# Tile pairs with one multiply, 16 tiles transposed on VectorE and loaded by quarters, and plain tiles loaded far ahead, in a matmul with rotary embedding

## The chip, the cores and the metric

One core of one Trainium2 chip; the other cores are idle. Times are microseconds on the device, of whole executions. A profile's span, from the first to the last instruction, is 1.7 to 1.8 us shorter than the time of the same execution. Engines: PE is TensorE, DVE VectorE, ACT ScalarE, POOL GpSimd, SP SyncE, which here only issues DMAs. A suffix q (SPq, ACTq) stands for an engine's instruction queue where it issues DMAs.

## The reference

```python
# x (16, 512, 768), weight (768, 768), cos and sin (512, 64), 12 heads; all float32
y = np.matmul(x, weight).reshape(batch, seq, n_heads, 64)
y1, y2 = y[..., :32], y[..., 32:]
out1 = y1 * cos1 - y2 * sin1          # cos1, sin1: first halves, the same for all heads
out2 = y2 * cos2 + y1 * sin2
out = np.concatenate([out1, out2], axis=-1).reshape(batch, seq, hidden)
```

## The kernel before

64 tiles of 128 rows by 768. Each is loaded on SP, cast to fp16 on ScalarE, transposed on TensorE (six times 128x128, into PSUM), evicted by ScalarE, multiplied by the weights (12 matmuls), multiplied twice on VectorE (by cos and by the signed sin), added on GpSimd, and stored by a DMA that ScalarE issues.

```python
    def load(i):
        xss[i] = xpool.tile([P, H], FP32, tag="xs", name="xs")             # 11 buffers
        nc.sync.dma_start(out=xss[i], in_=xv[i // SB, i % SB])
    ...
    def transpose(i, eng):
        xc = x16.pop(i)
        pt = pt_pool.tile([P, NKT, P], FP16, tag="pt", name="pt")
        for kt in range(NKT):
            nc.tensor.transpose(pt[:, kt, :], xc[:, ts(kt, P)], ident)
        xTT[i] = tpool.tile([P, NKT, P], FP16, tag="xT", name="xT")
        copy(eng, xTT[i], pt)
    ...
    def store(i):
        nc.scalar.dma_start(out=ov_dram[i // SB, i % SB], in_=ovs.pop(i))
    ...
    for i in range(FIRST, NMB):
        if i + AHEAD - FIRST < NMB:
            load(i + AHEAD - FIRST)
        if i + 1 < NMB:
            transpose(i + 1, nc.scalar)
        if 4 < i + 2 < NMB:
            cast(i + 2, nc.scalar)
        if i < NMB - 1:
            for kt in range(NKT):
                mm(i, kt)
            rope_whole(i)           # two multiplies on VectorE, one add on GpSimd
            store(i - 3)
```

## Time and profile before

| | before |
|---|---|
| time | 168.62 us (3 runs, 168.53 to 168.65) |
| span of the profiled run | 166.9 us, granted clock 0.983 |
| TensorE busy | 153.6 us; no wait between 21.4 and 160.1 us |
| a tile in the steady stage | 2.285 us: 1.95 matmul, 0.34 transposes |
| DMA | 53.2 MB, 319 GB/s over the span |
| DMAs in the steady stage | two a tile: one load, one store, 384 KB each |

The lines behind this table are in the prediction.

### The profile page before, as it was taken

To read this page: it belongs to the slowest core of one execution; us is meant where nothing else is said; L and a number is where in the kernel's file an instruction comes from. 1 tells how busy PE (TensorE), PEld (TensorE's weight loads), DVE (VectorE), ACT (ScalarE), POOL (GpSimd) and SP (SyncE) were. 2 spreads that over 40 slices of the span, in tenths; PEclk is the share of its full clock that TensorE was granted. 3 is DMA by queue.
4 is the path that set the end of the run, shared out by engine and by line. 5 is a ranking of instruction groups with operands and counts; after the bars stand their busy time and mean duration, and the time that the engine had idled before them with its cause. 6 is when DMAs were issued, how large, how long until landed. Compare 5 with 4: busy or idle time off the path is not lost.

```text
span 166.9 us, 3136 instructions
## 1 busy us (share of the span) xinstructions
PE 153.6 (92%) x1165; PEld 98.5 (59%) x1165; DVE 122.9 (74%) x142; ACT 97.9 (59%) x127; POOL 114.4 (69%) x67
## 2 busy tenths in 40 slices
PE   7657699999999999999999999999999999999930
PEld 2224466666666666666666666666666666666610
DVE  0522598777877688877778877778877778777792
ACT  3053366667766667766667766667666667666400
POOL 0000099777787777887777887777887777877770
PEclk9987999999999999999999999999999999999997
DMA  4999999999999999999999999999999984345544
GB/s 128 405 402 403 403 404 369 301 375 406 340 372 343 328 350 345 350 326 381 335 327 370 347 330 351 337 327 361 368 349 350 300 323 170 146 161 192 213 166 188
DMA packets 19887, 53.19 MB, mean 319 GB/s; under 512 B 2336, under 2 KB 2848, under 8 KB 19872
## 3 DMA queue, kind: packets, MB, share of 16 engines
q1 hardware_dynamic: 10368, 27.92, 49.5%
q10 hardware_dynamic: 9504, 25.07, 37.8%
q8 instruction: 9, 0.15, 0.5%
q14 instruction: 6, 0.05, 0.1%
HBM read 27.82 MB, written 25.17 MB: 317 GB/s over the span
## 4 chain that ended last, share of the span: by engine, by line
PE 88%; DMA 4%; ACT 2%; DVE 2%; issue 1%; SPq 1%; DVEq 0%
PE psy L103 74%; PE pt L93 13%; DMA xs<-in_x_dram 4%; PE psy L216 1%; DVE ov L130 1%; ACT xc L69 1%; ACT xT L69 1%; DVE qv L122 1%; SPq L80 1%; DVE tv L116 0%; SPq L75 0%; DVEq L130 0%; DVEq L116 0%
## 5 line engine op out<-in xcount | busy, mean ns | idle before, releaser
L130 POOL TENSOR_TENSOR ov<-tv,qv 128x768 f32<-128x768 f32 x63 | 114.2, 1816 | 47.4 <-DVE qv L122 46.2
L103 PE MATMUL psy<-w_sb,xT 128*128 128x512 f16 x756 | 135.1, 329 | 2.5 <-ACT xT L69 1.8
L103 PEld LDWEIGHTS <-xT 128*128 128x128 f16 x756 | 71.8, 99 | 44.9 <-ACT xT L69 2.1
L116 DVE TENSOR_TENSOR tv<-psy,cos_sb 128x768 f32<-128x768 f32 (+1 forms) x65 | 61.4, 944 | 31.7 <-PE psy L103 30.5
L69 ACT COPY xT<-pt 128x768 f16<-128x768 f16 x63 | 50.3, 798 | 51.2 <-PE pt L93 51.2
L122 DVE TENSOR_TENSOR qv<-psy,tee_sb 128x768 f32<-128x768 f32 (+1 forms) x65 | 60.7, 934 | 0.0
L69 ACT CAST xc<-xs 128x768 f16<-128x768 f32 x63 | 52.7, 836 | 5.8 <-DMA xs<-in_x_dram 5.8
L93 PE MATMUL pt<-ident,xc 128*128 128x128 f16 x384 | 31.9, 219 | 2.9 <-ACT xc L69 2.2
L93 PEld LDWEIGHTS <-xc 128*128 128x128 f16 x384 | 26.6, 98 | 12.3 <-ACT xc L69 3.0
L83 DVE CAST w_sb<-w_raw 128x768 f16<-128x768 f32 x6 | 3.3, 558 | 4.1 <-DMA w_raw<-in_weight_dram 4.1
L141 PE MATMUL cold_ps<-cold 128*128 128x512 f16 x13 | 4.6, 514 | 1.2 <-DVE cold L146 1.2
L141 PEld LDWEIGHTS <-cold 128*128 128x128 f16 x13 | 1.5, 126 | 3.3 <-issue 1.9
L71 DVE CAST xc<-xs 128x768 f16<-128x768 f32 x1 | 0.6, 560 | 3.7 <-DMA xs<-in_x_dram 3.7
L69 ACT ACT_TABLE_LOAD x1 | 1.3, 1283 | 2.1 <-issue 2.1
L216 PE MATMUL psy<-w_sb,xT 128*128 128x384 f16 x12 | 2.1, 326 | 0.0
L130 DVE TENSOR_TENSOR ov<-tv,qv 128x384 f32<-128x384 f32 x2 | 1.7, 862 | 0.1
L216 PEld LDWEIGHTS <-xT 128*128 128x128 f16 x12 | 1.2, 98 | 0.8
L71 DVE COPY xT<-pt 128x768 f16<-128x768 f16 x1 | 0.6, 556 | 0.6 <-PE pt L93 0.6
L146 DVE MEMSET cold<- 128x256 uint32 x1 | 0.3, 272 | 0.9 <-PEq L244 0.9
L244 POOL MEMSET const-float32-0.0<- 128x1 f32 x1 | 0.1, 98 | 0.2 <-issue 0.2
L185 DVE TENSOR_SCALAR tee_sb<-tee_sb 128x128 f32<-128x128 f32 x1 | 0.2, 220 | 0.0
L244 POOL MEMSET const-bfloat16-1.0<- 128x1 bf16 x1 | 0.1, 101 | 0.0
(2 smaller groups left out, 0.2 us busy)
## 6 DMA issues: line engine op xcount, KB each, us to landing
xs<-in_x_dram SPq DMA_DIRECT2D x64, 384.0 KB, 5.6
out_dram<-ov ACTq DMA_DIRECT2D x63, 384.0 KB, 4.8
w_raw<-in_weight_dram SPq DMA_DIRECT2D x6, 384.0 KB, 5.9
out_dram<-ov SPq DMA_DIRECT2D x2, 192.0 KB, 2.2
cos_sb<-in_cos_dram ACTq DMA_DIRECT2D x1, 128.0 KB, 5.2
tee_sb<-in_sin_dram ACTq DMA_DIRECT2D x1, 128.0 KB, 6.2
ident<-identity ACTq DMA_DIRECT2D x1, 32.0 KB, 3.6
```

What stands on the lines that cost most here:

```text
L69: eng.copy(out=o, in_=i_)
L71: eng.tensor_copy(out=o, in_=i_)
L80: nc.sync.dma_start(out=w_raw[:, kt], in_=wv[:, kt])
L83: nc.vector.tensor_copy(out=w_sb[:, kt], in_=w_raw[:, kt])
L93: nc.tensor.transpose(pt[:, kt, :], xc[:, ts(kt, P)], ident)
L103: nc.tensor.matmul(psys[i][:, ds(noff, nsz)], xTT[i][:, kt, :], w_sb[:, kt, ds(noff % H, nsz)], start=(kt == 0), stop=(kt == NKT - 1),)
L116: nc.vector.tensor_tensor(out=tv.rearrange("p (h d) -> p h d", d=D), in0=ps.rearrange("p (h d) -> p h d", d=D), in1=cos_sb[:, sb, :].unsqu ...
L122: nc.vector.tensor_tensor(out=qv.rearrange("p (h t d) -> p h t d", t=2, d=HD), in0=ps.rearrange("p (h t d) -> p h t d", t=2, d=HD)[:, :, : ...
L130: add_eng.tensor_tensor(out=ov[:, ds(c0, n)], in0=tv, in1=qv, op=ADD)
L141: nc.tensor.matmul(cold_ps, cold[:, 0:P], cold, start=True, stop=True)
L146: nc.vector.memset(cold, 0.0)
L216: nc.tensor.matmul(psys[i][:, n, 0:sz], xTT[i][:, kt, :], w_sb[:, kt, ds(c0, sz)], start=(kt == 0), stop=(kt == NKT - 1),)
```

## The change

Its intent: take TensorE transposes off the engine that bounds the kernel. VectorE transposes 16 tiles within 32x32 blocks, on pairs of fp16 seen as one fp32. For that a tile is put into SBUF by quarters of the hidden dimension, so it is loaded by four DMAs of 32 partitions. VectorE gets the time for it from one multiply per pair of tiles, by cos and sin at once, in place of four. The start loads four x tiles ahead of the weights, and early on plain tiles are loaded up to 14 pairs ahead. Cut to the core:

```diff
+    def by_blocks(n, s):                      # pair n, tile s of it
+        return s == 1 and 6 < n < NP - ALONE and n % SB != 0
...
-    xpool = ctx.enter_context(tc.tile_pool(name="xpool", bufs=AHEAD + 3))
+    xpool = ctx.enter_context(tc.tile_pool(name="xpool", bufs=24))
+    bpool = ctx.enter_context(tc.tile_pool(name="bpool", bufs=AHEAD_B + 1))
...
+    def load_blocks(n):
...
+        src = x[b].rearrange("(j a r) (q k) -> r q a j k", r=SB, a=R, q=NQ)
+        dst = xss[n, 1].rearrange("p (j k) -> p j k", j=NQ)
+        for q in (0, 2, 1, 3):
+            eng = nc.sync if q < 2 else nc.scalar
+            eng.dma_start(out=dst[ts(q, R)], in_=src[r, q])
...
+    def transpose_blocks(n, s):
+        xT = tpool.tile([P, NT, P, 2], FP16, tag="xT", name="xT")
+        nc.vector.transpose(
+            out=xT.bitcast(FP32).rearrange("p t m e -> p (t m e)"),
+            in_=x16.pop((n, s)).bitcast(FP32),
+        )
...
+    def rope_pair(n):
+        rope(n, 0, 2 * H, psys[n].rearrange("p b n -> p (b n)"))   # one multiply, 3072 columns
+        add(n, 0, 2 * H, nc.gpsimd)
...
+    for n in range(2, NP):
+        while loaded < min(NP, n + 6 + max(0, AHEAD - n // 3)):
+            load_plain(loaded)
+            loaded += 1
+        if n + 1 < NP and by_blocks(n + 1, 1):
+            transpose_blocks(n + 1, 1)
+        for s in (0, 1):
+            for c in CHUNKS:
+                mm(n, s, *c)
+            upto("turn", 2 * n + s + 3)          # transposes on TensorE, evictions on ScalarE
+            upto("cast", 2 * n + s + 5)
...
+        if n >= 3:
+            store(n - 3, nc.scalar)              # a pair, 768 KB
+        load_blocks(n + AHEAD_B)
+        if n < NP - ALONE:
+            rope_pair(n)
```

## The prediction

What the prediction told of the hardware and no trace or run of this case shows is cut from it, and each cut is marked. The sum came to a span of 150.9 + 7.3 = 158.2 us and, with 1.7 us over it, to 159.9, put down as 159.8. Three things are estimates: that the cast and the weight loads cost no more with strided reads, that transfers of 32 partitions run at the rate of full ones, and that GpSimd slows nothing of VectorE in the tail.

> **What bounds the kernel now.** I read the busy shares first, then the chain of work that ended last, then the same chain in order of time, and the timeline of the first and last 12 us. The shares and the chain:
>
> ```profile
> PE 153.6 (92%) x1165; PEld 98.5 (59%) x1165; DVE 122.9 (74%) x142; ACT 97.9 (59%) x127; POOL 114.4 (69%) x67
> DMA  4999999999999999999999999999999984345544
> ...
> PE 88%; DMA 4%; ACT 2%; DVE 2%; issue 1%; SPq 1%; DVEq 0%
> ```
>
> TensorE is the bound, and nothing else comes near it on the chain. The DMA row looks just as full, and I come back to it. In order of time the chain has three stages:
>
> ```profile
> 15.84 3.10 PE psy L103 x18
> 18.93 0.35 PE pt L93 x6
> 19.33 0.67 issue
> 20.00 0.84 ACT xc L69
> 20.89 0.51 PE pt L93 x6
> 21.40 1.95 PE psy L103 x12
> 23.35 0.34 PE pt L93 x6
> ...
> 158.17 1.96 PE psy L216 x12
> 160.70 0.56 DVE qv L122
> 161.28 1.17 DVE ov L130
> ```
>
> Start: until 21.40 us only three tiles are multiplied and five transposed. Steady stage: a tile costs 1.95 us of matmul and 0.34 us of transposes without a gap; 61 tiles x 1.953 + 59 x 0.338 = 139.1 us, which from 21.4 gives 160.5, and the chain has the last matmul end at 160.13. Tail: 160.13 to 166.9, 6.8 us. So there are three places to gain: the start, the 0.34 us per tile, the tail. The rest of the engines in the steady stage:
>
> ```profile
> L130 POOL TENSOR_TENSOR ov<-tv,qv 128x768 f32<-128x768 f32 x63 | 114.2, 1816 | 47.4 <-DVE qv L122 46.2
> L116 DVE TENSOR_TENSOR tv<-psy,cos_sb 128x768 f32<-128x768 f32 (+1 forms) x65 | 61.4, 944 | 31.7 <-PE psy L103 30.5
> L69 ACT COPY xT<-pt 128x768 f16<-128x768 f16 x63 | 50.3, 798 | 51.2 <-PE pt L93 51.2
> L69 ACT CAST xc<-xs 128x768 f16<-128x768 f32 x63 | 52.7, 836 | 5.8 <-DMA xs<-in_x_dram 5.8
> ```
>
> Of the 2.285 us per tile VectorE fills 1.9 (two multiplies), GpSimd 1.82, ScalarE 1.63: all wait for TensorE, none is far from it.
>
> The DMA row is not a bound yet. Loads alone ran at 402 GB/s; the demand of the steady stage is 786 KB per 2.285 us = 344 GB/s, and the windows of 4 us show 304 to 415. In the trace's packet records a 3 KB packet takes 121 ns in both queues, which for 16 engines is 406 GB/s; 6.6% of the load packets between 60 and 100 us take over 200 ns and make 26% of the load time. I read those as latency of a queue that had run empty, not as lost capacity. No cast waits for x after the start (5.8 us in two waits).
>
> [...]no transpose on VectorE is in this trace. [...]the first add of the last tile (two SBUF inputs) took 1.17 us beside a GpSimd add, the second 0.56 us alone; the multiplies (PSUM and SBUF) stay at 0.95 beside GpSimd. [...]the cast, which now reads pairs of fp32 at a step of 24 bytes[...]: I take the cast as unchanged. [...]All stationary operands of the transposes and those of the block tiles now have a step of 2 elements; the trace only has packed ones, 98 ns each[...]. I take them as unchanged.
>
> **The change part by part.**
>
> *Block transposes.* Pairs 7 to 27 without those divisible by 4 give 16 tiles. Each drops 6 TensorE transposes, 0.338 us on the path: 16 x 0.338 = -5.4 us. Each drops an eviction of 0.80 us on ScalarE, off the path. Each adds one VectorE transpose of 384 fp32: from the multiplies of 768 (0.95 us) and 384 (0.55 us) a column costs 1.03 ns and an instruction 0.16 us, so 0.56 us (an estimate[...]), beside TensorE.
>
> *One multiply per pair.* 3072 columns in place of 4 x 768: 0.16 + 3072 x 1.03 = 3.32 us against 3.80. VectorE per pair with a block tile: 3.32 + 0.56 = 3.88 us of TensorE's 2 x 1.953 + 0.338 = 4.24 us (4.58 without). It fits, with 0.36 us to spare. The PSUM now has two pair buffers: pair n+1 may start when the multiply of pair n-1 is done, 3.32 us after that pair's last matmul; it would start 4.24 us after it. Slack 0.9 us, so no stall. This saves nothing by itself; it pays for the transposes.
>
> *GpSimd.* One add of 1536: at most 2 x 1816 = 3.63 us of 4.24. One input is now read with halves swapped; unchanged rate assumed.
>
> *ScalarE.* Per pair with a block tile 2 x 0.84 + 0.80 + three DMA issues at 0.34 = 3.5 us of 4.24.
>
> *Start.* Order of loads: four x tiles, six weight rows, then cos and sin. Before, x0 was there at 4.83 and each later transfer 0.975 us after the one ahead (weight casts at 9.49, 10.46, and 12.41, 13.39). So w0 lands at 4.83 + 4 x 0.975 = 8.7 and w5 at 13.6, as before. By then 4 tiles are transposed, and each weight needs 0.56 us of cast and at most 3 x 0.325 us of matmul, so TensorE keeps pace: w5 cast by 14.2, matmuls to 15.1, (1,0)'s last to 15.5. The third x pair comes after cos and sin (0.65 us): 15.2, cast 16.05, transposed 16.4. So the fourth tile starts at about 16.4 with five tiles transposed, the very state that the kernel before had at 21.40: -5.0 us. Risk: before, the clock was at half from about 11 to 14.4 us:
>
> ```profile
> PEclk9987999999999999999999999999999999999997
> 10.81 3.80 PE psy L103 x12
> ```
>
> Twelve matmuls took 3.80 us in place of 1.95. The change keeps TensorE warm with extra matmuls, but 7 to 9.3 us is thin; if the slow stretch comes again it costs up to 1.7 us. I add 0.8.
>
> *Steady stage.* 61 x 1.953 + 43 x 0.338 = 133.7 us. From 16.4 + 0.8: last matmul at 150.9.
>
> *Tail.* All transposes are done early, so the last six tiles come every 1.95 us; VectorE needs 0.16 x 2 + 1536 x 1.03 = 1.9 us for each and starts 1.4 us behind (3.32 - 1.95), so it ends some 1.0 us behind. Then three instructions on 512 columns (0.69 each) and three on 256 (0.42): 3.3 us[...]. From the last add (163.97) to the end before were 2.97 us. Tail 1.0 + 3.3 + 3.0 = 7.3, against 6.8: +0.5.
>
> *Sum.* Span 150.9 + 7.3 = 158.2. The time is 1.7 us over the span (168.62 to 166.9): 159.9. I say 159.8; the parts are -5.4, -5.0 + 0.8, +0.5.
>
> **The rivals.** *DMA becomes the bound.* With block tiles the demand is 1.573 MB per 4.24 us = 371 GB/s, and a 768-byte packet should take about 36 ns (1 KB takes 46, 1.5 KB takes 66, 3 KB 121), so 19% more for a quarter-loaded tile: 388 GB/s of 406. For: that is tight[...]. Against: 24 buffers in place of 11 let 13 tiles (5.1 MB) be read ahead, which over some 90 us takes 56 GB/s off[...].[...]
>
> *VectorE or the PSUM becomes the bound.* If the transpose takes 1.0 us rather than 0.56, VectorE needs 4.32 us per block pair, and 16 x 0.1 plus waits cost 2 to 4 us: 163.[...]
>
> *Strided reads cost.* If the cast at a 24-byte step took twice as long, ScalarE would need 5.3 us a plain pair and the kernel would be no faster (170 or more). If strided weight loads doubled a transpose, 48 x 0.34 = 16 us would undo everything: 174. [...]an author who kept this layout over six transposes per tile would have seen it.
>
> *GpSimd.* If swapped halves cost 20%, 4.36 us a pair makes it the bound for 16 pairs: 2 to 3 us.
>
> **Range and chances.** Downward little is left: without the cold stretch and with VectorE on time in the tail 158; so low 156.5. Upward several of the rivals are each worth 2 to 5 us: high 165. Two rivals would make it the same or slower, together some 9%: faster 0.91, same 0.05, slower 0.04.
>
> **What would show it.** Right: the chain stays with TensorE, at about 4.24 us per block pair and 4.58 per plain pair; the first matmul of tile (1,1) at 16 to 18 us; the multiply at 3.3, the transpose at 0.56, the cast at 0.84, the add at 3.6 us or less; weight loads at 98 ns. Wrong: TensorE waiting for the pair multiply or for a cast in pairs 7 to 27 (VectorE, or quarters landing late), a cast over 1 us, an add over 4.2 us, a slow clock after 20 us.

## The result and the profile after

| | before | after |
|---|---|---|
| time | 168.63 us (4 runs, 168.53 to 168.75) | 176.93 us (4 runs, 175.81 to 177.39) |
| ratio of fast runs | | 1.048, 95% interval 1.043 to 1.053 |
| span, granted clock | 166.9 us, 0.983 | 174.9 us, 0.958 |
| TensorE without work between 22 us and its last matmul | 0.0 us | 9.8 us |
| lost there to a low clock | 0.0 us | 4.8 us |

The result is right in its numbers and slower by 4.8%. Ratios here and below are the mean time of one kernel's fast runs over that of the other's of the same rounds, so not quite the ratio of the medians that are quoted. The last two rows are sums over windows of 1 us: the part of a window in which TensorE was not busy, and its busy part times what the granted clock lacked.

The page of the changed kernel, busy shares, slices and chain (four lines of them):

```profile
PE 154.4 (88%) x1074; PEld 94.8 (54%) x1074; DVE 123.8 (71%) x74; ACT 87.5 (50%) x109; POOL 109.2 (62%) x38
...
PE   7899999995895799999689999999999699999900
...
PEclk9999999999699699999969999999999999999995
...
DMA 42%; PE 38%; DVE 6%; ACT 3%; issue 2%; ACTq 2%; SPq 2%; POOL 1%; POOLq 1%; DVEq 0%
```

TensorE has holes at 42, 55, 86 and 139 us, the first three with a dip of the clock behind them: waits of 2.51, 2.89 and 2.00 us were followed by 12 matmuls in 3.58, 3.74 and 3.54 us in place of 2.11, at a granted clock of down to 0.50; after the wait of 1.52 us at 139 us they took 2.11, and in e2 the clock stayed at 1.00 after one of 2.3 us (85.4 to 87.7 us). The chain, 88% TensorE before, now runs over DMAs for 42% of the span. The pieces that were changed did what was expected of them; the groups of instructions by shape:

```profile
L194 POOL TENSOR_TENSOR ov<-tq 128x1536 f32<-128x1536 f32 x29 | 100.2, 3458 | 60.7 <-DVE tq L183 47.7 <-DMA out_dram<-ov 13.0
L183 DVE TENSOR_TENSOR tq<-psy,csn 128x3072 f32<-128x3072 f32 x29 | 97.3, 3356 | 35.1 <-PE psy L169 35.1
L76 ACT CAST xc<-xs 128x768 f16<-128x768 f32 x46 | 40.8, 901 | 8.3 <-DMA xs<-in_x_dram 7.9 <-issue 0.3
L126 PEld LDWEIGHTS <-xc 128*128 128x128 f16 x288 | 20.2, 100 | 11.6 <-ACT xc L76 4.4 <-DVE xc L78 1.2 <-issue 1.1
L133 DVE STREAM_TRANSPOSE xT<-xc 128x384 f32<-128x384 f32 x16 | 9.1, 570 | 2.4 <-ACT xc L76 2.4
```

The column behind the first bar is busy time and mean ns. The multiply takes 3.36 us (3.32 worked out), the block transpose 0.57 (0.56), the add 3.46 (at most 3.63), a strided weight load 100 ns (98 packed), the cast 0.90 (0.84 taken). So did the start; the chain in order of time:

```profile
15.72 0.90 ACT xc L76
...
16.66 0.51 PE pt L126 x6
17.17 1.95 PE psy L169 x12
19.12 0.34 PE pt L126 x6
```

The fourth tile starts at 17.17 us, where 16.4 and 0.8 in reserve had been written. The half-speed stretch before 20 us is gone: between 11 and 14 us the granted clock was 0.50 and is 1.00. From 7 to 11 us TensorE was busy for 42% of the time before, and for 87% in the change.

One hole in detail, from the timeline of the changed kernel (start, duration, instruction; in brackets the idle time of the engine before it and what ended it):

```profile
52.47 0.50 PE L126 MATMUL pt<-ident,xc 128*128 128x128 f16 x6
52.80 2.11 PE L169 MATMUL psy<-w_sb,xT 128*128 128x256 f16 x12
...
54.83 0.41 ACTq L240 DMA_DIRECT2D out_dram<-ov  x1
...
55.28 1.63 ACTq L102 DMA_DIRECT2D xb<-in_x_dram  x2
...
56.95 0.80 ACT L76 COPY xT<-pt 128x768 f16<-128x768 f16 x1 [4.65 <-DMA xs<-in_x_dram]
57.65 0.89 ACT L76 CAST xc<-xs 128x768 f16<-128x768 f32 x1
57.81 3.74 PE L169 MATMUL psy<-w_sb,xT 128*128 128x512 f16 x12 [2.89 <-ACT xT L76]
```

The transposes of a tile are done at 52.97 us. Their eviction, 0.80 us of work, starts only at 56.95, after ScalarE had been idle for 4.65 us; TensorE waits 2.89 us for it, and its next 12 matmuls take 3.74 us, where the 12 above took 2.11, at the low clock (0.50 from 58 to 61 us). ScalarE did not wait for the data of the eviction. Ahead of it in its order stand a store and two quarter loads, and it could not issue them: by the single records of the trace, 2.46 of the 4.65 us passed before the store could be issued and 0.83 before the second quarter could; the three issues themselves took 1.21. The list of the compiled program shows why; first one DMA of SP, then five instructions of ScalarE in order:

```
SP   L83  DMACopy xs_637<-in_x_dram 128x768        [waits DMAHW6, Activation]
...
ACT  L76  TensorCopy xc_625<-xb_519 128x768        [waits DMAHW5, DMAHW6, DMAHW0, Activation]
ACT  L240 DMACopy out_0_dram<-ov_466 128x2x768     [waits DMAHW6, Pool]
ACT  L102 DMACopy xb_628<-in_x_dram 32x4x192       [waits DMAHW1]
ACT  L102 DMACopy xb_628<-in_x_dram 32x4x192       [waits DMAHW3]
ACT  L76  TensorCopy xT_661<-pt_654 128x768        [waits PE]
```

The program has eight completion counters for DMAs, DMAHW0 to 7. They go to the DMAs in turn, in the order of the compiled list, over both queues, and a DMA is not issued until the one eight before it has landed. (All 155 DMAs take the counters in turn, and for each of the 147 after the first eight its engine waits, at it or earlier, for the DMA eight before.) The list is not in the order of the kernel's text: SP's DMAs run ahead of ScalarE's in it. The store takes counter 6 from the load of `xs_637`, which the text issues after the store. The chain in order of time has that load in flight until the store's issue:

```profile
48.62 6.14 DMA xs<-in_x_dram
...
54.83 6.18 DMA out_dram<-ov
...
61.09 6.10 DMA out_dram<-ov
```

Load, store, store: each issue follows the landing of the DMA whose counter it takes. In a stage of four pairs the changed kernel has 4 stores, 5 plain loads and 12 quarters, 21 DMAs in 17.3 us (8 x 1.953 + 5 x 0.338), so on average a DMA must land within 8/21 x 17.3 = 6.6 us of its own issue, or the one that takes its counter is late; the medians to landing are 5.2 to 6.6 us, single ones up to 9.4. Before, it was 16 DMAs in 18.3 us: 9.1 us, with medians of 4.8 and 5.6.

### The profile page after: what moved, and what is told of

It reads as the page before. It is cut to its first block, busy times and chain, and to the rows that moved or that the text cites. A ratio compares the mean times of both kernels' runs of the same rounds, so it can differ in the third digit from the quotient of the medians.

```text
span 174.9 us, 2708 instructions
## 1 busy us (share of the span) xinstructions
PE 154.4 (88%) x1074; PEld 94.8 (54%) x1074; DVE 123.8 (71%) x74; ACT 87.5 (50%) x109; POOL 109.2 (62%) x38
## 4 chain that ended last, share of the span: by engine, by line
DMA 42%; PE 38%; DVE 6%; ACT 3%; issue 2%; ACTq 2%; SPq 2%; POOL 1%; POOLq 1%; DVEq 0%
PE psy L169 32%; DMA out_dram<-ov 16%; DMA xb<-in_x_dram 13%; DMA xs<-in_x_dram 9%; DVE tq L183 6%; PE pt L126 5%; DMA w_raw<-in_weight_dram 4%; ACT xc L76 2%; ACTq L102 1%; POOL ov L194 1%; POOLq L364 1%; ACT xT L76 1%; SPq L83 1%; ACTq L240 1%; SPq L102 1%
## 5 line engine op out<-in xcount | busy, mean ns | idle before, releaser
L194 POOL TENSOR_TENSOR ov<-tq 128x1536 f32<-128x1536 f32 (+1 forms) x34 | 109.0, 3216 | 60.7 <-DVE tq L183 47.7
L169 PE MATMUL psy<-w_sb,xT 128*128 128x512 f16 (+1 forms) x744 | 133.8, 334 | 7.8 <-ACT xT L76 7.8
L183 DVE TENSOR_TENSOR tq<-psy,csn 128x3072 f32<-128x3072 f32 (+2 forms) x35 | 102.6, 2943 | 35.1 <-PE psy L169 35.1
L76 ACT COPY xT<-pt 128x768 f16<-128x768 f16 x46 | 36.5, 799 | 51.3 <-PE pt L126 25.4
L76 ACT CAST xc<-xs 128x768 f16<-128x768 f32 x46 | 40.8, 901 | 8.3 <-DMA xs<-in_x_dram 7.9
L126 PE MATMUL pt<-ident,xc 128*128 128x128 f16 x288 | 24.3, 223 | 3.0 <-ACT xc L76 2.3
L126 PEld LDWEIGHTS <-xc 128*128 128x128 f16 x288 | 20.2, 100 | 11.6 <-ACT xc L76 4.4
L76 ACT CAST xc<-xb 128x768 f16<-128x768 f32 x16 | 14.4, 899 | 7.3 <-DMA xb<-in_x_dram 4.5
L133 DVE STREAM_TRANSPOSE xT<-xc 128x384 f32<-128x384 f32 x16 | 9.1, 570 | 2.4 <-ACT xc L76 2.4
L169 PE MATMUL psz<-w_sb,xT 128*128 128x512 f16 (+1 forms) x24 | 4.2, 326 | 0.0
```

Of the source, the lines that this page charges most:

```text
L76: eng.copy(out=o, in_=i_)
L126: nc.tensor.transpose(pt[:, t, e, :], xc[:, t, e, :], ident)
L133: nc.vector.transpose(out=xT.bitcast(FP32).rearrange("p t m e -> p (t m e)"), in_=x16.pop((n, s)).bitcast(FP32),)
L169: nc.tensor.matmul(ps, xTT[n, s][:, t, e, :], w_sb[:, t, e, lo:hi], start=((t, e) == CHUNKS[0] and not joined), stop=((t, e) == CHUNKS[-1] ...
L183: nc.vector.tensor_tensor(out=tqs[n][:, :, c0:c1].rearrange("p j (h d) -> p j h d", d=D), in0=ps.rearrange("p (h d) -> p h d", d=D) .unsqu ...
L194: eng.tensor_tensor(out=ovs[n][:, ds(c0, w)].rearrange("p (h t d) -> p h t d", t=2, d=HD), in0=tq[:, 0].rearrange("p (h t d) -> p h t d", ...
```

## The experiments

They ran four at a time, each four on one chip, the fours on four different chips (e1 to e4; f1, f2, e5 and h1; f3, j1, j2 and g1; k1 to l2), with the kernel before beside them at medians of 166.8 to 167.1 us. The change itself was not run beside them, so runs of different fours, and the change, are compared by their ratios (the change: 1.048). Theories: **A**, the counters; **B**, slow transfers (packets of 768 bytes, or 32 partitions); **C**, VectorE and the two PSUM buffers too tight; **D**, the far look-ahead, which makes the SP queue deep. (Two counts in the expectations are off: 6.25 DMAs a pair counts quarters for every pair, the stage has 21 in four pairs, 5.25 a pair; and g1 goes from 21 to 19, not from 25 to 23. The 2.0 us from span to time is 1.8 in the runs.) With one core a run is called slow by its time alone. In e1, e3 and k2 half the runs are slow, and the profiled runs of e1 and k2 are among them, so there a slow run may be one in which a stall came and a fast one one in which it did not.

**e1_one_plain**, wrong result:

```diff
-        for q in (0, 2, 1, 3):
-            eng = nc.sync if q < 2 else nc.scalar
-            eng.dma_start(out=dst[ts(q, R)], in_=src[r, q])
+        nc.sync.dma_start(out=xss[n, 1], in_=x[b].rearrange("(p r) h -> r p h", r=SB)[r])
```

> Wrong result on purpose: each of the 16 block tiles is loaded by one transfer of whole 3 KB rows on the SP queue in place of four quarters; cast, VectorE transpose, matmuls and buffers as in the change. Theory A (counters): the instruction list shows that every DMA, of both queues, takes the next of eight completion counters in program order, and its issue waits until the DMA eight before it has landed; four quarters use up four of the eight, so SP and ScalarE stop at issues. With 3.0 in place of 6.25 DMAs a pair the stalls of TensorE after 40 us vanish: 17.2 + 133.7 + 7.3 us span + 2.0 = 160 us. Rival B (packets of 768 B or 32 partitions make transfers slow): also about 160. Rival C (VectorE and the two PSUM buffers are too tight): stays at 173 to 177. Rival D (plain loads far ahead fill the queues): 168 or more.

166.24 us (163.29 to 167.97; the fast runs 165.7 and 163.3), ratio 0.986 (0.975 to 0.996). C falls: with the same VectorE work and the same PSUM buffers, 6% of the time (1.048 to 0.986), some 10 us, is gone. A was too sure of itself: TensorE is still idle for 4.2 us in the profiled run, a slow one, where ScalarE waits 6.8 us once.

**e2_four_whole_rows**, wrong result: four DMAs of 32 partitions, but whole rows of 3 KB.

```diff
-            eng.dma_start(out=dst[ts(q, R)], in_=src[r, q])
+            eng.dma_start(out=xss[n, 1][ts(q, R)], in_=src[ts(q, R)])   # src: rows of 768
```

> Wrong result on purpose: four transfers of 32 partitions on the same queues and in the same order as in the change, but of whole 3 KB rows, so there are no small packets. Theory A (eight counters): as slow as the change, 172 to 178 us. Rival B in its form of small packets: about 160 us; in its form of 32 partitions: slow as A says, which e3 and a later run must part.

175.37 us, ratio 1.052 (1.045 to 1.058); TensorE idle for 11.0 us. As slow as the change without one small packet.

**e3_one_small_packets**, wrong result: one DMA of 128 partitions in pieces of 768 bytes.

```diff
+        src = x[b].rearrange("(p j) (q k) -> q p j k", j=SB, q=NQ)[r]
+        nc.sync.dma_start(out=xss[n, 1].rearrange("p (j k) -> p j k", j=NQ), in_=src)
```

> Wrong result on purpose: one transfer of 128 partitions in four pieces of 768 B each, so small packets as in the change but one counter a tile. Theory A: 160 to 162 us, as e1. Rival B (small packets): near the change, 170 us or more.

165.13 us (fast runs 163.33 and 163.97), ratio 0.981 (0.973 to 0.988). Small packets alone do no harm. A's 160 to 162 us was missed here too: TensorE is idle once, for 1.8 us. In the packet records they take 36 ns, as the prediction had interpolated.

**e4_no_blocks**, correct: `by_blocks` returns False, all else kept.

> Correct result: no block tiles; all tiles transposed on TensorE and loaded plainly, the rest of the change kept (pairs, start, loads far ahead). TensorE has 17.2 + 61 x 1.953 + 59 x 0.338 = 156.3 us, tail 7.3, and 2.0 over the span: 165.6 us under A and B. Under C (pair multiply and PSUM) or D (loads far ahead) it stalls: 170 or more.

170.13 us, ratio 1.018 (1.011 to 1.025). 4.5 us over the sum that A gave, and without a quarter in it. The profile shows one hole, at 57 us: a load that SP had issued at 45.58 took 11.66 us to land, and the store that takes its counter held up ScalarE till 57.26. So quarters are not needed for such a stop; this spoke for D as well.

**f1_near**, correct: the change without the far look-ahead.

```diff
-        while loaded < min(NP, n + 6 + max(0, AHEAD - n // 3)):
+        while loaded < min(NP, n + 6):
```

> Correct result: the change without the far look-ahead of plain loads (pair n+6 is loaded at pair n throughout; the first eight pairs as before); quarters kept. e1, e3 and e4 still stalled TensorE once or twice, behind a store whose counter had last been taken by a load that stood in a deep SP queue. Theory A+D (counters, made worse by the deep queue): fewer stalls than the change, 165 to 172 us. A alone, if only the four quarters matter: 173 to 177. If the look-ahead is what keeps the transfers in time: 178 or more.

173.32 us (fast runs 172.5 to 173.5), ratio 1.036 (1.033 to 1.039), TensorE idle for 9.7 us. The look-ahead is not the cause; by the ratios, 1.048 and 1.036, it costs some 2 us at most.

**f2_near_one_plain**, wrong result: f1 and e1 together.

> Wrong result on purpose: f1 with each block tile loaded by one plain transfer, as in e1. Theory A+D: no stall is left, 17.2 + 133.7 + 8.7 (the tail as e4 showed it) + 2.0 = 161.6 us. If the stalls left in e1 have another cause than the look-ahead: 163 to 166, as e1.

160.79 us (160.49 to 160.97), ratio 0.963 (0.961 to 0.964), TensorE idle for 0.0 us after 22 us. With neither quarters nor the long look-ahead the prediction's 159.8 us holds within 1 us. Part of that is luck: the last matmul ends 0.8 us before the predicted 150.9, the tail is 1.3 us longer, and the ratio forecast was 0.948, as the kernel before is faster on this chip.

**e5_four_columns**, wrong result: four DMAs of all 128 partitions and 192 columns.

```diff
+        src = x[b].rearrange("(p r) (q k) -> r q p k", r=SB, q=NQ)
+        dst = xss[n, 1].rearrange("p (q k) -> p q k", q=NQ)
...
+            eng.dma_start(out=dst[:, q], in_=src[r, q])
```

> Wrong result on purpose: the change with four transfers a block tile, each of all 128 partitions and 192 columns (768 B packets), on the same queues in the same order. Theory A (counters): as slow as the change and e2, 172 to 178 us, as the count is the same. Rival B in its form of 32 partitions: 163 to 166 us, as e3.

175.39 us, ratio 1.051 (1.044 to 1.057). With e2 and e3 this ends B in both forms: neither packets nor partitions matter. What e2 and e5 share with the change, and e3 does not, is four DMAs a tile, two of them issued on ScalarE; j2 below keeps the four and moves the issues.

**h1_before_four**, correct: the kernel before, x loads from tile 8 on in four column pieces.

```diff
-        nc.sync.dma_start(out=xss[i], in_=xv[i // SB, i % SB])
+        k = H // 4 if i >= AHEAD else H
+        for c in range(0, H, k):
+            nc.sync.dma_start(out=xss[i][:, ds(c, k)], in_=xv[i // SB, i % SB, :, ds(c, k)])
```

> Correct result: the kernel before with every x load from tile 8 on split into four transfers of 192 columns on the SP queue; nothing else. Five DMAs a tile of 2.285 us take counters, so a DMA must land within 1.6 tiles, 3.7 us, where it took 4.8 to 5.6. Theory A: slower by 3% or more, with ScalarE waiting at its stores. Rival B (32 partitions) and any theory of the changed kernel alone: same within 1%.

190.89 us, ratio 1.140 (1.134 to 1.146). ScalarE issues the same stores as before, and nothing else; still it now stops in front of evictions until a piece of x has landed. Waits of its ScalarE:

```profile
ACT xT L69 <- PE pt L97: 33.7, 42, 2.8
ACT xT L69 <- DMA xs<-in_x_dram: 29.4, 16, 2.6
```

(us in total, times, longest). An eviction has no business with a load of x; between them stands only the counter of a store. The size of the loss is not the counters' alone: SP's own issues are 12% of this chain.

**g1_near_double**, correct: f1 with plain tiles of two pairs in one DMA of 768 KB (the 24 buffers become 14 and 5 double ones).

```diff
+            xd = dpool.tile([P, 2, H], FP32, tag="xd", name="xd")
+            nc.sync.dma_start(out=xd, in_=x[b].rearrange("(p r) h -> p r h", r=SB)[:, r : r + 2])
+            xss[n, s], xss[n + 1, s] = xd[:, 0], xd[:, 1]
```

> Correct result: f1 with plain tiles of two neighbouring pairs loaded by one transfer of 768 KB from pair 8 on, which takes a stage of four pairs from 25 to 23 counters (12 of them quarters, 4 stores). Theory A: a little faster than f1, 169 to 173 us. If the transfers' size matters more than their number: same as f1 or slower.

172.01 us, ratio 1.030 (1.024 to 1.037). Two DMAs fewer of 21 change nothing clear of noise against f1 (1.033 to 1.039).

**f3_near_no_blocks**, correct: f1 and e4 together.

> Correct result: pairs and the new start alone, no block tiles and no far look-ahead. f2 ran without stalls at 160.8; six transposes more for 16 tiles are 16 x 0.34 = 5.4 us: 166.2 us, a little less than the kernel before. If pairs cost something that f2 hides, 168 or more.

170.69 us, ratio 1.018 (1.009 to 1.027). A miss by 4.5 us: the hole of e4 is there again, so it is not the look-ahead's, and a store alone on ScalarE can still meet a late load. (The profile puts this wait down to GpSimd; but a load landed at 57.37 us, ScalarE's wait for a counter ended at 57.39, and its store was issued at 57.44.)

**j1_near_all_sp** and **j2_far_all_sp**, correct: f1 and the change, with every quarter and every store of a pair issued on SP. The edit of j2 is this and nothing more:

```diff
-            eng = nc.sync if q < 2 else nc.scalar
+            eng = nc.sync
...
-            store(n - 3, nc.scalar)
+            store(n - 3, nc.sync)
...
-    store(NP - 3, nc.scalar)
-    store(NP - 2, nc.scalar)
+    store(NP - 3, nc.sync)
+    store(NP - 2, nc.sync)
```

> Correct result: f1 with all quarters and all stores of pairs issued on SP, so ScalarE never stops at an issue; the number of DMAs and the eight counters are the same as in f1 (173.3). If the cost of waiting for a counter is that ScalarE, which casts and evicts, stands still: 160 to 164 us. If the eight counters limit the flow of data itself: 170 or more, with ScalarE waiting for x at its casts.

> Correct result: the change as it is, with the far look-ahead, but all quarters and stores of pairs on SP. If ScalarE standing still is the cost: 160 to 166 us. If the look-ahead also makes SP wait for buffers in front of quarters and stores: 166 to 172, stores late and GpSimd waiting for an output buffer.

161.36 us, ratio 0.966 (0.960 to 0.971), and 161.28 us, ratio 0.965 (0.959 to 0.971). The number of DMAs, the eight counters, the bytes and the small packets are those of the change; ScalarE no longer issues them. One more thing differs, in the compiled lists: with one queue the counters follow the kernel's text. In the change 22 of the 64 DMAs that ScalarE issues after the start take their counter from a DMA that the text issues later (f1 30, h1 51 of 63, e4 13 of 32, f3 17 of 32); in j1 and j2 none does. No run changes this order alone. It is not enough by itself for a stall: f2 has 15 of 32, the kernel before 7 of 63, and neither stalls. The slices of j2's page, against those of the change above:

```profile
PE   7899999999999999999999999999999999999700
...
PEclk9999999999999999999999999999999999999995
```

And the waits of ScalarE, in the changed kernel between 20 and 150 us and in j2 over the whole span:

```profile
ACT xT L76 <- PE pt L126: 20.8, 22, 2.6
ACT xT L76 <- DMA out_dram<-ov: 9.2, 3, 4.9
ACT xT L76 <- DMA xb<-in_x_dram: 5.8, 2, 3.0
ACT xT L76 <- DMA xs<-in_x_dram: 4.6, 1, 4.6
```

```profile
ACT xT L76 <- PE pt L126: 30.5, 35, 1.9
ACT xc L76 <- DMA xb<-in_x_dram: 12.3, 9, 2.4
ACT xc L76 <- DMA xs<-in_x_dram: 8.3, 2, 5.2
```

Evictions (`xT`) that began only after some DMA had landed, 19.6 us in six waits, are gone (4.0 of the 19.6 us were ScalarE's issuing itself, the rest waiting). Casts (`xc`) now wait for their own data, 12.3 us in nine short waits, which costs TensorE 0.4 us. SP waits for the counters too, but SP has nothing else to do. So the counters cost j2 next to nothing; yet little is left, as its chain shows:

```profile
DMA 43%; PE 32%; SPq 7%; DVE 7%; issue 3%; ACT 2%; POOL 1%; POOLq 1%; ACTq 0%; DVEq 0%
```

Loads, stores and quarters that follow one another by counters make a path about as long as TensorE's; in f2, without quarters, TensorE has 77% of the chain.

**k1_quarters_sp** and **k2_stores_sp**, correct: j2 with only one kind moved to SP.

> Correct result: the change with all four quarters issued on SP, the stores left on ScalarE. If the quarters' issues on ScalarE are most of the cost: 162 to 166 us. If one stop at a store per pair is enough, as e4 and f3 (stores alone on ScalarE) suggest with their 4 to 5 us over the sum: 168 to 175.

> Correct result: the change with the stores of pairs issued on SP, the quarters left as they are, two on SP and two on ScalarE. If the stores' issues on ScalarE are most of the cost: 162 to 166 us. If the quarters' are: 168 to 175.

163.0 us, ratio 0.974 (0.968 to 0.980), with the stores left on ScalarE; 165.56 us (fast runs 164.2 and 162.9), ratio 0.977 (0.967 to 0.987), with half of the quarters left there. Both intervals overlap, and neither kind is "most of the cost" by itself: either move ends most of the stops. In both profiles (k2's is of a slow run) no eviction waits for a DMA any more, though 32 DMAs are still issued on ScalarE. In both, too, none of these takes its counter from a DMA that the text issues later; so the order in which the counters are handed out may be what counts, which no run has tested alone.

**l1_no_blocks_all_sp**, correct: j2 without block tiles.

> Correct result: j2 without block tiles (all tiles transposed on TensorE, loaded plainly). j2's 161.3 plus 16 x 0.34 = 5.4 us: 166.7 us. More means that pairs or the look-ahead still stall; less means that the block transposes are worth less than their matmuls.

167.17 us, ratio 0.999 (0.993 to 1.005). Against j2's 161.28, which ran on another chip, the 16 block transposes are worth 5.9 us, or 5.6 by the two ratios (0.999 and 0.965 of 167), where 5.4 had been worked out. It also says that all else in the change, pairs, start and look-ahead together, is worth nothing on these chips.

**l2_before_stores_sp**, correct: the kernel before with `nc.sync.dma_start` in `store`.

> Correct result: the kernel before with its stores issued on SP. Its TensorE runs without a gap from 21.4 us on, so there is nothing to gain: the same within 0.5%. If it gains 2% or more, the gain of j2 is not the change's.

168.41 us, ratio 1.004 (0.995 to 1.013): no gain. What j2 gains over the kernel before is the change's own.

## Why the prediction was wrong

Predicted 159.8 us, in 156.5 to 165 (the parts, as listed there, add up to 159.5); measured 176.93.

**The step that failed** is "ScalarE. Per pair with a block tile 2 x 0.84 + 0.80 + three DMA issues at 0.34 = 3.5 us of 4.24". It counts an issue as 0.34 us of work. The work alone is more: issues take 0.40 us (a store) and 0.53 (a quarter) on average, casts 0.90, so 2 x 0.90 + 0.80 + 0.40 + 2 x 0.53 = 4.1 of 4.24 us. And in the changed kernel an issue can also be a wait for a DMA that landed late, and everything behind it in ScalarE's order waits with it. ScalarE stood idle for 19.6 us in six such waits in front of evictions; TensorE lost 9.8 us to idleness and 4.8 us to the low clock that followed, 14.6 of the 15.5 us by which its last matmul came late (about 166.4 against 150.9). The trace of before held the hint: in the waits of SP's queue, loads wait for stores to land:

```profile
SPq L75 <- DMA out_dram<-ov: 6.0, 2, 5.2
```

That view was asked for before the prediction, which does not mention it, as nothing in the kernel before suffered from it; it counts bytes, not DMAs.

**The rivals, one by one.** "DMA becomes the bound" was the nearest, and for the wrong reason: I asked for GB/s and packets. The packet of 768 bytes takes its 36 ns, e3 shows it does no harm, and j2 moves the same bytes in 160.0 us of span, though by then a path over DMAs is as long as TensorE's (43% of its chain). "VectorE or the PSUM", "Strided reads" and "GpSimd" did not happen: no time above came from them once ScalarE was free (f2, j2). The strided cast costs 0.90 in place of 0.84 on ScalarE, beside other work (on VectorE, which does two, 0.95 in place of 0.56; why, no run shows).

**The mechanism that was right.** With free issues (j2) the fourth tile and the rate are where the sum had them; the last matmul comes at about 151 us, as predicted. The block transposes are worth what was said (l1 against j2).

**A term mis-sized: the tail.** Predicted 7.3 us from last matmul to end, measured 8.5 in the changed kernel and 8.8 in j2. The timeline of j2's end:

```profile
142.63 12.31 POOL L194 TENSOR_TENSOR ov<-tq 128x1536 f32<-128x1536 f32 x6 [1.12 <-DVE tq L183]
...
151.16 0.69 DVE L218 TENSOR_TENSOR tq<-psy,csn 128x512 f32<-128x512 f32 x1
...
153.88 0.42 DVE L222 TENSOR_TENSOR ov<-psy,tq 128x256 f32<-128x256 f32 x1
154.97 0.37 ACTq L240 DMA_DIRECT2D out_dram<-ov  x1
```

VectorE is done at 154.3 us, 3.2 us after the last matmul, where 4.3 had been reckoned. From there to the end 3.0 us were reckoned, as before, and 5.7 passed: GpSimd, which I had left out of the tail, has six adds in a row of 12.31 us and ends at 154.94, 0.6 us after VectorE; the store of its last add is issued then and takes 4.0 us to land, where the last two stores of the kernel before took 2.2.

**A term that depends on the chip: the start.** The start did gain 4.2 us (21.40 to 17.17), but l1 is no faster than the kernel before beside it: 1.1 us of idle TensorE (one wait for a pair multiply of VectorE) and 1.9 us of longer tail (8.7 against 6.8) take most of it back, and on those chips most fast runs of the kernel before took 166.4 to 167.2 us with a granted clock of up to 0.996, against 168.6 at 0.983. That these lack the half-speed stretch at the start is inferred from the clock: there is no trace of one. l2's trace, at 168.41 us and 0.984, has the stretch at 11.0 to 14.4 us as before; at the granted clock of 0.50 these 3.4 us cost up to 1.7, by an estimate.

What stays open: how much of h1's loss is the counters' and how much SP's issue time; and how much of j2's gain comes from a free ScalarE and how much from counters in the order of the text. That k1 and k2 keep 2.7 and 5.1 us of idle TensorE has a cause that their traces show: ScalarE stands in front of the cast of a block tile whose quarters have not landed (3.3 and 4.1 us in k1, 3.3 and 2.9 in k2), and the next eviction or cast comes behind it.

## What to carry to other kernels

Count DMAs, not only bytes: with a fixed number of completion counters handed out in turn, as the eight of this program, a DMA's issue waits for another DMA, and the time allowed is the stage's time times the number of counters over its DMAs (here 17.3 x 8/21 = 6.6 us, where single DMAs took up to 9.4). Look in the compiled list whose counter a DMA takes: it can be that of one which the text issues later (here for 22 of 64). Issue DMAs from an engine that computes nothing, if one has room (here the ratio went from 1.048 to 0.965, j2); on one that also evicts or casts, a late counter stops its work, and the loss is then to be found on a third engine (here 19.6 us of waits on ScalarE, 9.8 us without work on TensorE). When a change adds instructions to an engine's queue, ask of each what it can wait for, and look at the queue's own waits before predicting.
